# Another order for the steps of the attention in a one-core decoder kernel

## The chip, the cores and the metric

The kernel runs on one core of a Trainium2 chip, in one launch. The metric is the device time of the program in microseconds (us). The five instruction streams that matter are TensorE (PE, matmuls; PEld is its weight load), VectorE (DVE), ScalarE (ACT), GpSimd (POOL) and SyncE (SP, which only issues transfers). Each takes its instructions in the order in which they stand in its queue, and an instruction whose input or buffer isn't ready holds up all that stand behind it.

## The reference, cut to what matters

A decoder trunk of two layers over 256 tokens of width 1024, in float32. Each layer has a feed-forward network (FFN) before and after a mixer, each followed by a LayerNorm. The mixer of the first layer is a gated recurrence, that of the second an attention in which 16 heads of width 64 look back in three dilated windows (groups). All three groups share one key and one value; each has its own query. The change touches only this attention:

```
q = (x @ w_q).reshape(bsz, s, N_GROUPS, N_HEADS, HEAD_DIM)
for g, (window, dilation) in enumerate(DILATION_PAIRS):
    o, l = dilated_group(q[:, :, g], k, v, slopes, window, dilation)   # softmax over the window's keys
    outs.append(o); lses.append(l)
wts = softmax(stack(lses, axis=0), axis=0)
out = sum(wts[..., None] * stack(outs, axis=0), axis=0)
return out.reshape(bsz, s, N_HEADS * HEAD_DIM) @ w_o
```

The weighted sum over the three groups is the same as one softmax over the keys of all three, and so the kernel computes it: exps of three groups, one sum, one division.

## The kernel before

All weights come from memory in pieces of 128x1024 float32 (512 KB). A piece is loaded into a tile `raw`, and is then split into a rounded part `w_hi` (line 127, a cast on ScalarE) and the remainder `w_lo` (line 128, on VectorE); each product is made of three matmuls, hi x hi, hi x lo, lo x hi (line 90). There are 4 buffers for `raw` and 10 for the split pieces. `pump` (line 139) loads and splits the next piece, `take` (line 145) hands out the oldest split one.

The attention runs over 8 pairs of heads. It is written as steps, and the text `ATTENTION` (line 620) names them in order; a step is a letter and a number. Inside the attention ScalarE, VectorE and GpSimd keep this order (`pinned`, line 152), and so do all matmuls (line 88): the text alone says in which order each engine meets its work.

| step | what it does | engine, line |
|---|---|---|
| `pv` | next weight piece: transfer, cast, remainder (`pV`: the cast on VectorE too) | SP 126, ACT 127, DVE 128 |
| `r` | transposes the first queries, which were projected for two pairs at once | PE 98, ACT 665 |
| `U` n | query projection of pair n/3, group n mod 3: 24 matmuls, 128x256 | PE 88 |
| `Q` n | scales it and keeps it (frees U's bank) | ACT 665 |
| `F` p, `S` p | scores of pair p for the first and the second 128 tokens: 6 matmuls each | PE 88 |
| `M` h | adds the distances to the scores of head h and finds the extremum (frees the banks of F and S) | DVE 717 |
| `E` h | exp, with its sum | ACT 726 |
| `N` h | reciprocal of the sum; adds the three groups | DVE 733 to 735 |
| `L` h | scales by the reciprocal (`sg`, `hh`) | ACT 743 |
| `P` h, `C` h | three transposes; keeps their result (frees P's bank) | PE 98, DVE 754 |
| `O` p, `D` p | value sums of pair p, 4 matmuls; splits them in `o_hi` and `o_lo` (frees O's bank) | PE 88, ACT 104, DVE 105 |
| `J` n | a quarter of the output projection for one piece of `w_o`: 6 matmuls | PE 88 |

A head goes through F, S, M, E, N, L, P, C, and a pair then through O and D. Between them TensorE makes the query projections of later pairs, and behind the last of those the parts J. The results of U, F, P, O (and half of the last S) take a bank each of the four named `mm`; the two double banks `yy` hold S, and from J0 on the output projection.

`T` at the end of the text gives the numbers of pieces that are issued in `finish` (line 279), which computes the rest of the projection with the LayerNorm: the first ahead of it, the second behind the first add of the LayerNorm (line 237), the third behind its scaling (lines 249 and 250). Then the LayerNorm's rows are transposed (line 254), split into `xT` (lines 104, 105), and the last FFN begins.

Of the kernel before, what the change touches and what calls it, by code (L numbers as in the profile page):

```python
# [46 lines left out]
def trunk_kernel(  # L47
# [397 lines left out]
    def natural_pair(turn_x, then):  # L445


        later = []
        for t, ps in enumerate(natural_both(turn_x)):
            tmp = act.tile([P, 512], F32, name="nat", tag="o_hi", bufs=4)  # L450
            nc.scalar.copy(tmp, ps)

            def rest(t=t, tmp=tmp):
                pt = bank()
                for m in range(4):
                    turn(pt[:, m * P:(m + 1) * P], tmp[:, m * P:(m + 1) * P])
                then(t, pt.rearrange("p (m s) -> p m s", m=4))
            later.append(rest)
        return later
# [157 lines left out]
    def kv_duo():  # L617
        return [act.tile([P, 2, SEQ], F32R, name="kv", bufs=KVBUFS) for _ in range(2)]

    ATTENTION = """pv pV U2 Q2 pv r0 pv r1 U5 Q5 F0 S0 U6 M0 pv pv E0 N0 M1 U7 L0 P0 E1 Q7 pv U8 N1 C0 Q6 F1 S1 U9 L1 M2  # L620
        pv E2 P1 U10 C1 Q8 M3 O0 N2 E3 N3 L2 Q10 U11 P2 pv D0 C2 pv F2 S2 L3 M4 Q11 E4 Q9 N4 U12 L4 P3 C3 U13
        O1 U14 Q12 M5 E5 pv pv pv N5 P4 L5 F3 S3 C4 Q13 D1 M6 U15 pv E6 P5 Q14 C5 U16 M7 O2 Q15 pv E7 N6 L6
        U17 P6 N7 L7 D2 pv Q17 F4 S4 C6 M8 pv P7 Q16 E8 C7 U18 N8 L8 M9 Q18 pv O3 E9 U19 D3 pv F5 S5 P8 N9 C8
        L9 Q19 U20 M10 P9 Q20 E10 C9 N10 M11 U21 pv L10 U22 Q21 pv P10 E11 Q22 N11 C10 U23 O4 pv F6 S6 pv pv
        D4 M12 Q23 pv E12 N12 L11 L12 P11 C11 M13 J0 O5 pv P12 J4 E13 N13 C12 D5 L13 F7 S7 P13 J3 M14 E14 J7
        N14 L14 C13 O6 J11 M15 E15 P14 C14 N15 J8 pv J2 D6 L15 P15 J1 C15 O7 J6 pv J5 D7 T20100""".split()
    ATTENTION_TAIL = ((3, 0), (2, 1), (3, 1)), ((3, 1), (2, 0), (3, 0))

    def keys_values(turn_x):
# [23 lines left out]
    def attention(kv, ln_i, turn_x):  # L653
# [134 lines left out]
        rest = natural_pair(turn_x, first)  # L788
        for s in ATTENTION:
            if s[0] == "p":  # L790
# [115 lines left out]
```

## Time and profile before

| | us |
|---|---|
| three runs | 1064.87, 1065.18, 1067.47 (median 1065.18) |
| profiled execution | 1063.59 |
| its span, first to last instruction | 1061.5 |
| TensorE busy | 1033.7 (97%) |
| VectorE busy | 649.8 (61%) |
| ScalarE busy | 525.5 (50%) |
| GpSimd busy | 11.9 (1%) |

The profile is of one execution; 2.1 us of it lie around the span. Matmuls overlap, so a busy TensorE isn't TensorE at its peak. The attention (from U2 to the transposes of its LayerNorm) lies at 737 to 864 us of the span. In a timeline a row gives the start, the time that the instructions took, the engine, the line, the operation with output and inputs, and in brackets how long the engine sat idle before it and which instruction ended that. In the chain of waits, which is followed back from the last instruction, a row is a start, a length and what the program's end hung on.

### The profile page before, as it was taken

What the parts mean: (1) busy time and instruction counts of PE and PEld (TensorE: products, weight loads), DVE (VectorE), ACT (ScalarE), POOL (GpSimd) and SP (SyncE); (2) the same over time, 40 slices, a digit from 0 to 9 for tenths busy, and PEclk for the clock granted to TensorE, in tenths of its full rate; (3) what the DMA queues carried; (4) which work ended last, traced back from release to release, by engine and by line L of the source; (5) the groups of instructions that cost most, each with busy time, mean ns of one, the idle gap of its engine ahead of it and who ended that gap; (6) DMA issues with size and microseconds to landing.
All of it is one profiled execution on the core that took longest, in us unless ns stands there. A gap on an engine that the chain in (4) does not pass through costs nothing.

```text
span 1061.5 us, 13737 instructions
## 1 busy us (share of the span) xinstructions
PE 1033.7 (97%) x5305; PEld 869.0 (82%) x5305; DVE 649.8 (61%) x847; ACT 525.5 (50%) x730; POOL 11.9 (1%) x18
## 2 busy tenths in 40 slices
PE   9999999999899999999999999999998889999997
PEld 7888888899778888887988888888888778888885
DVE  5765555685886455557645545557776887554544
ACT  6664443369745444343534444433765745443430
POOL 0000000000000000000000000000000000000000
PEclk9999999999999999999999999999999999999999
DMA  8885555185358565652856555461432547555521
GB/s 295 279 290 184 198 176 182 65 281 183 113 197 274 177 198 172 205 176 90 295 183 216 182 189 197 160 199 54 146 121 99 179 139 266 203 178 206 179 99 40
DMA packets 55648, 192.69 MB, mean 182 GB/s; under 512 B 6432, under 2 KB 6688, under 8 KB 55584
## 3 DMA queue, kind: packets, MB, share of 16 engines
q1 hardware_dynamic: 55584, 191.83, 53.4%
q8 instruction: 41, 0.67, 0.3%
q14 instruction: 23, 0.19, 0.1%
HBM read 190.75 MB, written 1.05 MB: 181 GB/s over the span
## 4 chain that ended last, share of the span: by engine, by line
PE 85%; ACT 6%; DVE 6%; issue 1%; DMA 1%; POOL 0%; SPq 0%; DVEq 0%; ACTq 0%; POOLq 0%
PE mm L88 54%; PE yy L88 28%; PE mm L98 3%; DVE w_lo L128 2%; ACT w_hi L127 2%; ACT sc L726 1%; ACT th L101 1%; ACT L101 1%; DMA raw<-in_q_w_dram 0%; DVE sc L717 0%; DMA raw<-in_w_in_dram 0%; DVE sc L735 0%; DVE xn L237 0%; ACT aa L101 0%; DVE st L238 0%
## 5 line engine op out<-in xcount | busy, mean ns | idle before, releaser
L128 DVE TENSOR_TENSOR w_lo<-raw,w_hi 128x1024 fp32r<-128x1024 f32 (+1 forms) x343 | 413.5, 1220 | 222.1 <-ACT w_hi L127 212.1
L88 PE MATMUL mm<-w_hi,xT 128*128 128x512 f32 x1536 | 494.2, 394 | 1.8 <-DVE xT L105 1.8
L127 ACT CAST w_hi<-raw 128x1024 fp32r<-128x1024 f32 (+1 forms) x342 | 354.2, 1049 | 238.5 <-PE yy L88 112.1
L88 PEld LDWEIGHTS mm<-w_hi,xT 128*128 128x128 f32 x1536 | 288.5, 188 | 63.6 <-DVE xT L105 3.8
L88 PE MATMUL mm<-w_lo,xT 128*128 128x512 f32 x768 | 299.8, 390 | 1.0 <-DVE w_lo L128 1.0
L88 PEld LDWEIGHTS mm<-w_lo,xT 128*128 128x128 f32 x768 | 144.5, 188 | 30.8 <-DVE w_lo L128 2.1
L88 PE MATMUL yy<-w_hi,h_hi 128*128 128x512 f32 x352 | 138.3, 393 | 0.0
L88 PE MATMUL yy<-w_hi,h_lo 128*128 128x512 f32 x352 | 137.2, 390 | 0.0
L88 PE MATMUL yy<-w_lo,h_hi 128*128 128x512 f32 x352 | 137.0, 389 | 0.0
L347 ACT ACTIVATE sg<-mm 128x256 f32<-128x256 f32 x88 | 33.7, 383 | 153.7 <-PE mm L88 153.3
L350 DVE SCALAR_TENSOR_TENSOR gated<-mm,sg 128x256 f32<-128x256 f32 x88 | 36.8, 420 | 106.6 <-ACT sg L347 106.6
L88 PE MATMUL mm<-xT,w_hi 128*128 128x256 f32 x480 | 89.9, 289 | 2.8 <-ACT q L665 2.6
L88 PEld LDWEIGHTS mm<-xT,w_hi 128*128 128x128 f32 x480 | 75.7, 194 | 5.3 <-ACT q L665 2.8
L88 PEld LDWEIGHTS yy<-w_hi,h_lo 128*128 128x128 f32 x352 | 66.1, 188 | 13.9
L88 PEld LDWEIGHTS yy<-w_lo,h_hi 128*128 128x128 f32 x352 | 66.2, 188 | 13.3
L88 PEld LDWEIGHTS yy<-w_hi,h_hi 128*128 128x128 f32 x352 | 66.1, 188 | 13.3
L88 PE MATMUL mm<-xT,w_lo 128*128 128x256 f32 x240 | 68.5, 285 | 0.0
L88 PEld LDWEIGHTS mm<-xT,w_lo 128*128 128x128 f32 x240 | 46.5, 194 | 0.0
L104 ACT CAST xT<-mm 128x512 fp32r<-128x512 f32 x20 | 11.7, 586 | 60.4 <-PE mm L98 60.3
L88 PE MATMUL yy<-xT,w_hi 128*128 128x256 f32 x224 | 41.2, 286 | 0.0
L105 DVE TENSOR_TENSOR h_lo<-mm,h_hi 128x512 fp32r<-128x512 f32 x44 | 30.3, 689 | 13.0 <-ACT h_hi L104 13.0
L88 PEld LDWEIGHTS yy<-xT,w_hi 128*128 128x128 f32 x224 | 35.1, 192 | 0.2
(109 smaller groups left out, 709.8 us busy)
## 6 DMA issues: line engine op xcount, KB each, us to landing
raw<-in_w_in_dram SPq DMA_DIRECT2D x175, 512.0 KB, 4.5
raw<-in_w_out_dram SPq DMA_DIRECT2D x88, 512.0 KB, 5.0
raw<-in_q_w_dram SPq DMA_DIRECT2D x20, 512.0 KB, 4.0
raw<-in_rg_in_dram SPq DMA_DIRECT2D x16, 512.0 KB, 4.9
gb<-in_ln_dram SPq DMA_DIRECT2D x24, 256.0 KB, 5.9
raw<-in_rg_out_dram SPq DMA_DIRECT2D x10, 512.0 KB, 4.0
raw<-in_v_w_dram SPq DMA_DIRECT2D x8, 512.0 KB, 4.8
raw<-in_k_w_dram SPq DMA_DIRECT2D x8, 512.0 KB, 5.3
```

The source lines that it names most:

```text
L88: tc.keep_in_program_order(nc.tensor.matmul(ps, lhsT=lhsT, rhs=rhs, start=start, stop=stop))
L98: tc.keep_in_program_order(nc.tensor.transpose(ps, src, ident))
L101: tc.keep_in_program_order(nc.scalar.activation(dst_, src, f, **kw))
L104: nc.scalar.copy(hi, src)
L105: nc.vector.tensor_tensor(lo, src, f32(hi), ALU.subtract)
L127: (nc.scalar.copy if high is nc.scalar else high.tensor_copy)(w[0][:, c], raw[:, c])
L128: i = low.tensor_tensor(out=w[1][:, c], in0=raw[:, c], in1=f32(w[0][:, c]), op=ALU.subtract)
L347: nc.scalar.activation(sg, ps[:, :256], AF.Silu)
L350: nc.vector.scalar_tensor_tensor(gated[j][:, t, :], ps[:, 256:], 0.5, sg, ALU.mult, ALU.mult)
L726: nc.scalar.activation(scs[h][:, :, c], scs[h][:, :, c], AF.Exp, bias=mns[h][:, t, 1:2], scale=-1.0, accum_out=den[:, t:t + 1])
```

## The change

Only the text of steps and the three numbers behind `T` change. The text has 209 steps before and after, among them the same 27 `pv` and one `pV`. No function changes.

```
-    ATTENTION = """pv pV U2 Q2 pv r0 pv r1 U5 Q5 F0 S0 U6 M0 pv pv E0 N0 M1 U7 L0 P0 E1 Q7 pv U8 N1 C0 Q6 F1 S1 U9 L1 M2
...
-        N14 L14 C13 O6 J11 M15 E15 P14 C14 N15 J8 pv J2 D6 L15 P15 J1 C15 O7 J6 pv J5 D7 T20100""".split()
+    ATTENTION = """pv pV U2 pv r0 r1 U5 Q2 F0 S0 U6 M0 pv pv E0 N0 U7 M1 Q5 pv pv L0 E1 P0 N1 C0 Q7 U8 F1 S1 Q6 U9 L1 M2
...
+        P13 J7 N14 C13 L14 J11 O6 P14 J8 C14 J2 D6 E15 N15 pv J1 L15 P15 C15 J5 pv O7 J6 D7 T12000""".split()
```

At `T` the pieces are 2, 0 and 1 before, and 1, 2 and 0 now. On TensorE few steps move: P3 stands ahead of U12, U20 ahead of P8, F6 ahead of U23, with S6 still behind O4, and at the end J4, J7, J11, J1 and J5 a place or two from where they were. SyncE and GpSimd keep their order. Most of what moves stands on ScalarE and VectorE. Three places:

ScalarE around L9, the scaling of head 9 (its exps are `sc_6876` before and `sc_6866` now; `q_6895` before and `q_6891` now are U19's query). Before:

```order
L726 ACTIVATE sc_6876,den_6892<-sc_6876,mn_6877 128x3x256
L104 CAST o_hi_6793<-mm_6887 128x256
L127 CAST w_hi_6924<-raw_6923 128x1024
L743 ACTIVATE sg_6955<-sc_6876,rd_6949 128x128
L743 ACTIVATE hh_6956<-sc_6876,rd_6949 128x256
L665 ACTIVATE q_6895<-mm_6896,qsc_104 128x256
L665 ACTIVATE q_6960<-mm_6961,qsc_104 128x256
L726 ACTIVATE sc_6986,den_6995<-sc_6986,mn_6987 128x3x128
L726 ACTIVATE sc_6986,den_6995<-sc_6986,mn_6987 128x3x256
```

And now:

```order
L726 ACTIVATE sc_6866,den_6888<-sc_6866,mn_6867 128x3x256
L104 CAST o_hi_6795<-mm_6877 128x256
L127 CAST w_hi_6966<-raw_6965 128x1024
L743 ACTIVATE sg_6971<-sc_6819,rd_6862 128x128
L743 ACTIVATE hh_6972<-sc_6819,rd_6862 128x256
L743 ACTIVATE sg_6983<-sc_6866,rd_6961 128x128
L743 ACTIVATE hh_6984<-sc_6866,rd_6961 128x256
L665 ACTIVATE q_6933<-mm_6934,qsc_104 128x256
L726 ACTIVATE sc_6979,den_6994<-sc_6979,mn_6980 128x3x128
L726 ACTIVATE sc_6979,den_6994<-sc_6979,mn_6980 128x3x256
L665 ACTIVATE q_6891<-mm_6892,qsc_104 128x256
```

L8 moved down to L9, Q20 ahead of E10, and Q19 behind E10.

ScalarE around E11 and E12, the exps of heads 11 and 12 (`sc_7004` and `sc_7160` before, `sc_7060` and `sc_7160` now). Before:

```order
L726 ACTIVATE sc_7004,den_7081<-sc_7004,mn_7005 128x3x256
L665 ACTIVATE q_7044<-mm_7045,qsc_104 128x256
L127 CAST w_hi_7123<-raw_7122 128x1024
L127 CAST w_hi_7145<-raw_7144 128x1024
L127 CAST w_hi_7151<-raw_7150 128x1024
L104 CAST o_hi_7156<-mm_7117 128x256
L665 ACTIVATE q_7091<-mm_7092,qsc_104 128x256
L127 CAST w_hi_7166<-raw_7165 128x1024
L726 ACTIVATE sc_7160,den_7171<-sc_7160,mn_7161 128x3x128
L726 ACTIVATE sc_7160,den_7171<-sc_7160,mn_7161 128x3x256
L743 ACTIVATE sg_7178<-sc_7004,rd_7085 128x128
L743 ACTIVATE hh_7179<-sc_7004,rd_7085 128x256
```

And now:

```order
L726 ACTIVATE sc_7060,den_7080<-sc_7060,mn_7061 128x3x256
L665 ACTIVATE q_7034<-mm_7035,qsc_104 128x256
L665 ACTIVATE q_6997<-mm_6998,qsc_104 128x256
L127 CAST w_hi_7100<-raw_7099 128x1024
L127 CAST w_hi_7132<-raw_7131 128x1024
L743 ACTIVATE sg_7137<-sc_7060,rd_7083 128x128
L743 ACTIVATE hh_7138<-sc_7060,rd_7083 128x256
L127 CAST w_hi_7155<-raw_7154 128x1024
L665 ACTIVATE q_7105<-mm_7106,qsc_104 128x256
L127 CAST w_hi_7166<-raw_7165 128x1024
L127 CAST w_hi_7172<-raw_7171 128x1024
L726 ACTIVATE sc_7160,den_7177<-sc_7160,mn_7161 128x3x128
```

L11 (`sg` and `hh` from E11's exps) moved from behind E12 to ahead of it; two casts now stand directly ahead of E12, and D4 has gone from there.

VectorE at the same place, from the second half of M12 on (`p_7190` before and `p_7196` now are C11's result). Before:

```order
L717 ISA sc_7160,mn_7161<-yy_7136,dst_103 128x3x256
L717 ISA mn_7161 128x1
L128 TENSOR_TENSOR w_lo_7167<-raw_7165,w_hi_7166 128x1024
L733 RECIPROCAL rd_7174<-den_7171 128x2
L734 TENSOR_TENSOR sc_7160<-sc_7160 128x384
L735 TENSOR_TENSOR sc_7160<-sc_7160 128x384
L754 COPY p_7190<-mm_7186 128x384
L717 ISA sc_7192,mn_7193<-mm_7129,dst_103 128x3x128
L717 ISA mn_7193 128x1
L717 ISA sc_7192,mn_7193<-yy_7137,dst_103 128x3x256
```

And now:

```order
L717 ISA sc_7160,mn_7161<-yy_7146,dst_103 128x3x256
L717 ISA mn_7161 128x1
L128 TENSOR_TENSOR w_lo_7167<-raw_7165,w_hi_7166 128x1024
L128 TENSOR_TENSOR w_lo_7173<-raw_7171,w_hi_7172 128x1024
L733 RECIPROCAL rd_7180<-den_7177 128x2
L734 TENSOR_TENSOR sc_7160<-sc_7160 128x384
L735 TENSOR_TENSOR sc_7160<-sc_7160 128x384
L717 ISA sc_7184,mn_7185<-mm_7089,dst_103 128x3x128
L717 ISA mn_7185 128x1
L717 ISA sc_7184,mn_7185<-yy_7147,dst_103 128x3x256
L717 ISA mn_7185 128x1
L754 COPY p_7196<-mm_7192 128x384
```

A second remainder stands ahead of N12, and C11 moved behind M13.

## Rows read from the trace of the kernel before

**Rows 1.** The page's part 1: busy us (share of the span), instructions.

```profile
PE 1033.7 (97%) x5305; PEld 869.0 (82%) x5305; DVE 649.8 (61%) x847; ACT 525.5 (50%) x730; POOL 11.9 (1%) x18
```

**Rows 2.** Timeline of TensorE, 745 to 850 us, rows with idle time.

```profile
753.17 0.33 PE L98 MATMUL mm<-ident,sg 128*128 128x128 f32 x1 [0.68 <-ACT sg L743]
...
785.21 0.48 PE L88 MATMUL mm<-k,q 64*128 64x128 f32 x2 [2.06 <-DVE p L754]
...
799.52 0.71 PE L88 MATMUL mm<-k,q 64*128 64x128 f32 x8 [0.38 <-ACT q L665]
...
814.17 0.51 PE L88 MATMUL mm<-xT,w_hi 128*128 128x256 f32 x2 [2.57 <-ACT q L665]
...
833.75 0.33 PE L98 MATMUL mm<-ident,sg 128*128 128x128 f32 x1 [2.67 <-ACT sg L743]
```

**Rows 3.** Chain of waits, 740 to 862 us: start, us, what.

```profile
742.48 4.82 DMA raw<-in_q_w_dram
...
753.51 1.52 ACT sc L726 x4
...
786.02 0.82 PE mm L88 x9
786.84 1.41 PE yy L88 x10
788.25 3.08 PE mm L88 x24
...
814.17 4.39 PE mm L88 x24
...
852.86 7.05 PE yy L88 x30
```

**Rows 4.** One window: engines' busy us (instructions), then the granted clock, DMA share, GB/s.

```profile
816.00:817.00 1.00, 1.00 (x6) 1.00 (x6) 0.00 (x0) 0.00 (x0) 0.00 (x0) 0.50 0.00 0
```

**Rows 5.** Timeline around the attention's LayerNorm, 859 to 869 us.

```profile
863.78 0.63 PE L98 MATMUL mm<-ident,xn 128*128 128x128 f32 x4 [1.16 <-DVE xn L250]
...
865.00 1.22 DVE L128 TENSOR_TENSOR w_lo<-raw,w_hi 128x1024 fp32r<-128x1024 f32 x1
...
868.18 0.73 PE L88 MATMUL mm<-w_hi,xT 128*128 128x512 f32 x2 [1.49 <-DVE xT L105]
```

**Rows 6.** Timeline ahead of F3, 778 to 786 us.

```profile
779.00 2.94 ACT L127 CAST w_hi<-raw 128x1024 fp32r<-128x1024 f32 x3
780.07 3.50 DVE L128 TENSOR_TENSOR w_lo<-raw,w_hi 128x1024 fp32r<-128x1024 f32 x3 [2.03 <-ACT w_hi L127]
783.48 0.16 DVE L733 RECIPROCAL rd<-den 128x2 f32<-128x2 f32 x1
...
784.61 0.55 DVE L754 COPY p<-mm 128x384 f32<-128x384 f32 x1
```

**Rows 7.** Timeline ahead of U20, 811 to 815 us.

```profile
812.96 0.40 ACT L743 ACTIVATE sg<-sc,rd 128x128 f32<-128x128 f32 x1 [2.48 <-DVE sc L735]
...
813.25 0.55 DVE L717 CUSTOM_DVE_ANT_1 sc<-mm,dst 128x384 f32<-128x384 f32 x1
...
813.67 0.45 ACT L665 ACTIVATE q<-mm,qsc 128x256 f32<-128x256 f32 x1
...
814.60 0.08 DVE L717 DVE_READ_ACCUMULATOR2_ANT mn<- 128x1 f32 x1
```

**Rows 8.** Timeline around E0, 745 to 755 us.

```profile
747.45 0.08 DVE L717 DVE_READ_ACCUMULATOR2_ANT mn<- 128x1 f32 x1
...
748.44 1.28 ACT L726 ACT_TABLE_LOAD   x1
749.74 0.62 ACT L726 ACTIVATE sc<-sc,mn 128x384 f32<-128x384 f32 x1
```

**Rows 9.** Timeline ahead of P11, 825 to 835 us: N11's second add, and L11.

```profile
826.24 0.56 DVE L735 TENSOR_TENSOR sc<-sc 128x384 f32<-128x384 f32 x1
...
833.31 0.39 ACT L743 ACTIVATE sg<-sc,rd 128x128 f32<-128x128 f32 x1
```

More of the change, by code (lines that the diff above doesn't have):

```diff
@@ L618, in kv_duo @@
         return [act.tile([P, 2, SEQ], F32R, name="kv", bufs=KVBUFS) for _ in range(2)]
-    ATTENTION = """pv pV U2 Q2 pv r0 pv r1 U5 Q5 F0 S0 U6 M0 pv pv E0 N0 M1 U7 L0 P0 E1 Q7 pv U8 N1 C0 Q6 F1 S1 U9 L1 M2
[L621 to L625, printed above, removed]
-        N14 L14 C13 O6 J11 M15 E15 P14 C14 N15 J8 pv J2 D6 L15 P15 J1 C15 O7 J6 pv J5 D7 T20100""".split()
+    ATTENTION = """pv pV U2 pv r0 r1 U5 Q2 F0 S0 U6 M0 pv pv E0 N0 U7 M1 Q5 pv pv L0 E1 P0 N1 C0 Q7 U8 F1 S1 Q6 U9 L1 M2
+        pv P1 E2 U10 Q8 M3 C1 O0 Q9 E3 U11 N2 N3 pv L2 Q10 P2 D0 pv C2 F2 S2 L3 P3 M4 E4 N4 Q11 M5 U12 C3 U13
+        pv L4 O1 U14 E5 P4 pv Q13 pv F3 N5 D1 S3 Q12 C4 M6 pv L5 U15 P5 U16 E6 M7 pv E7 C5 O2 N6 U17 Q15 N7
+        L6 P6 pv Q14 D2 L7 F4 S4 M8 P7 Q16 Q17 C6 E8 C7 U18 N8 M9 pv Q18 O3 pv E9 U19 F5 S5 U20 D3 N9 pv L8
+        P8 M10 L9 Q20 C8 P9 E10 U21 C9 Q19 N10 L10 U22 M11 pv pv P10 E11 N11 Q22 F6 C10 Q21 pv U23 pv L11 O4
+        S6 pv M12 Q23 pv pv E12 N12 M13 L12 P11 C11 D4 J0 J4 P12 O5 C12 E13 F7 S7 N13 D5 L13 J3 M14 M15 E14
+        P13 J7 N14 C13 L14 J11 O6 P14 J8 C14 J2 D6 E15 N15 pv J1 L15 P15 C15 J5 pv O7 J6 D7 T12000""".split()
     ATTENTION_TAIL = ((3, 0), (2, 1), (3, 1)), ((3, 1), (2, 0), (3, 0))
```

## The prediction

> **What bounds the kernel now.** I read the page's busy shares first: TensorE is busy 97% of the span [rows 1], so over the whole program little can be won. The change touches one stage, the attention, at 737 to 863 us. Second, therefore, the timeline of TensorE alone in that stage: every row with an idle time names what ended it. Between U2 and the last O there are nine such rows, 0.68, 0.20, 0.24, 2.06, 0.32, 0.38, 2.57, 2.67 and 0.19 us, in all 9.3 us; the ones that matter most stand in [rows 2]. Each costs some 0.25 us more than its idle time, since the array has to fill again (in the chain of waits step follows step without that loss [rows 3]): 9 x 0.25 = 2.3. [...] So the stage loses 9.3 + 2.3 + 1.3 = 12.9 us to its order. That is all that another order can win there; at its end 1.16 and 1.49 us more are lost around the LayerNorm [rows 5].
>
> **Durations for the sum**, start to start. TensorE: F 0.8, S 1.4, U 3.0 [rows 3], P 0.3; J is 6 of 30 matmuls in 7.05 us [rows 3], 1.4 to 1.5 with its start; O 0.8, as F. ScalarE: cast 0.98 (three in 2.94) [rows 6], E 1.52 [rows 3], L 0.71 (812.96 to 813.67) and Q 0.45 [rows 7]. VectorE: remainder 1.16 (three in 3.50), N 1.13 (783.48 to 784.61), C 0.5 [rows 6], M 1.43 (813.25 to 814.68) [rows 7]; D I take at 0.4, less than C, whose tile is larger. A weight piece lands 4.8 us after its raw buffer is free [rows 3].
>
> **The change part by part.** It adds and removes no instruction: casts, exps, matmuls and transfers are the same in number, and SP and POOL keep their rows. Only places move, so each term is a wait that goes or comes.
>
> Start (P0). Before, the sixth cast stood ahead of E0 and waited for its transfer until 747.3 [rows 3]; the table load and E0 came behind it [rows 8], and P0 waited 0.68 us. Now E0 stands ahead of that cast and starts when M0 ends (747.53 [rows 8]) and the table is there, about 747.7, two us earlier; two casts that go between E0 and L0 take the time back only partly (L0 at 751.5, not 752.7). P0 follows U7 at 752.3 without a wait: -1.2 with the second half of the transposes, which was late too. As E0, M1 and C0 come earlier, the small waits of U9 (0.20) and F2 (0.24) go as well: -0.7.
> The trace shows 1.28 us of table load and E0 0.02 us behind it [rows 8]. [...]
>
> F3 (2.06 and 0.32, in all 3.1 with filling). Before, it waited for a bank that C4 gave back: C4 stood behind three remainders and N5. Now D1 is put ahead of C4, and D1 gives the second bank. Counted from the end of M5: C3 0.5 and the first remainder to 1.7; the second follows a cast behind E5 (0.1 + 1.52 + 0.98 = 2.6) and ends at 3.8, the third at 4.95, N5 at 6.1, D1 at 6.45. TensorE has U13's rest 1.15, O1 0.8, U14 3.0, P4 0.3 = 5.25. So 1.2 us of waiting stay: -1.9. F4 (0.38): Q14 now stands ahead of D2, -0.6.
>
> U20 (2.57, filling and clock: 4.1 in all). It waited for the bank of Q19, which stood behind L9, and L9 waited for N9 [rows 7]. Now U20 stands ahead of P8 and takes the bank of O3, which D3 gives back some 1.5 us before: -4.1. Q19 moves behind E10, so the next banks are late: P9 waits for Q20 (0.35) and U21 for C8 (0.2): +0.55.
>
> P11 (2.67, with filling 3.1). N11's second add ended at 826.80, but L11 started only at 833.31 [rows 9]: it stood behind Q22, four casts, D4, Q23 and E12. Now L11 stands behind two casts only and ahead of E12; it ends 3 us before P11 wants it: -3.1. F6 is drawn ahead of U23, and its second bank comes from Q22, behind E11: +0.65.
>
> The last pairs, new waits. From the end of S6 (time 0): M12's second half ends at 0.95 and gives J0 its banks, TensorE is done with P11 at 0.3: +0.7. J0 and J4 end at 3.8. E12 now stands behind two casts, the second of which has its transfer at about 1.3 (its raw buffer is freed by a remainder 3.5 us before S6's end, and 4.8 us pass): cast to 2.3, E12 to 3.8, N12 to 5.0, L12's parts to 5.4 and 5.8. P12: +1.7. M13 stands ahead of C11: 5.0 + 1.43 + 0.47 = 6.9, TensorE waits with O5 from 6.05: +0.85. Behind P12 and O5 on TensorE stand F7 and S7, and M14 to C15 wait for those, so these waits reach the end in full. From F7 on VectorE and ScalarE keep ahead (O6 wants C13 at 14.7 and has it at 14.5, so its 0.19 goes, -0.4, by a margin of 0.2).
>
> The other moves I cost at nothing: P3 ahead of U12 and J1, J5 and J6 change places with steps whose inputs are over 1 us old, and a weight piece is still split five U steps (15 us) ahead of the U that takes it; if that cover were gone, a piece would cost its lateness at its U.
>
> Tail. One weight piece is issued ahead of the last projection and two behind its first quarter, where it was two and one. Two remainders (2.3) now lie between the two adds of the first LayerNorm, where VectorE had 1.3 free: the transposes wait 1.0 longer (+1.0 on the 1.16). In return the remainder at 865.00, which held back the xT that TensorE waited 1.49 for [rows 5], is gone from there: -1.1. Together 0.
>
> **Sum.** Waits that go: 1.2 + 0.7 + 3.1 + 0.6 + 4.1 + 3.1 + 0.4 = 13.2 (12.9 by the rows, the difference is rounding). Waits that come or stay: 1.2 + 0.55 + 0.65 + 0.7 + 1.7 + 0.85 = 5.65. Net 12.9 - 5.65 = 7.2, say -7 us. The profiled execution took 1063.6; it would take 1056.6. The median of the runs is 1.6 above it, so I predict 1065.2 - 7 = 1058.2. Bounds: no new wait at all gives -13 (1052); if each of the eleven places where a margin is under 0.5 us fails by 0.5, -7 + 5.5 = -1.5 (1063.7).
>
> **Rivals.**
> A. The gaps only move. Five of the nine waits are for a PSUM bank, there are still four, and the order of TensorE hardly changes. For it: F3, F6, P9 and U21 still wait in my own count. The price: if every bank wait returns in its old size, only P0, L11's and the clock's terms stay, 1.2 + 3.1 + 1.3 = 5.6, less the new chain waits 0.7 + 1.7 + 0.85 = 3.25: -2.4, 1062.8, which measures as no change (this kernel can tell 0.3%, 3.2 us). Against it: at U20 the bank was held by a place in a queue [rows 7], not by a lack of time. [...]
> B. Better: the chain at P12 and O5 is shorter than counted because the second transfer is in time (-1.0 at P12, and with it O5) and F3's cast is not late (-1.2): -9.5 to -10, 1055.5. Against: the cast at P0 waited for exactly such a transfer [rows 3].
> C. Slower: casts that wait for their transfers hold up the exps. The new order puts two casts ahead of each of E11, L11 and E12, and one ahead of the second xT cast in the tail. Four places; if a transfer takes x us instead of 4.8, each loses x - 4.8. It eats the gain of 7 at x = 6.6 and costs 3.2 us more than before from x = 7.4 on; at 7.6 the time is 1069.4. For it: transfers queue where four are freed at once. Against: 4.8 us was seen with the queue in use [rows 3].
> D. A new stop brings the clock down as after U20: +1.3 each. P12 and the LayerNorm's transposes now stop 1.7 and 2.2 us; stops of 2.06 and 2.67 us [rows 2] did not bring it down, so I count none; one would make 1059.5, within my own case.
>
> **How the numbers follow.** My forecast (1055.5 to 1061): 0.58. A (1061 to 1065): 0.20. B (under 1055.5): 0.12. C and whatever else ends above 1065: 0.10. Faster by over 0.3% (below 1062): all of mine and B, and a little under half of A: 0.58 + 0.12 + 0.08 = 0.78. Same: the rest of A and a part of C, 0.15. Slower 0.07. For 8 in 10 I leave out the slower cases and the best end: 1053.5 to 1064.
>
> **What would show it.** In the timeline of the changed kernel: P0, U20 and P11 without an idle time over 0.3 us; no stretch at 0.50 in the attention; F3 still waiting 1 to 1.5 us for VectorE's o_lo; P12 about 1.7 us for ScalarE; the wait ahead of the LayerNorm's transposes near 2.2 us, and the one behind them near 0.4. Wrong would be: casts waiting for a transfer over 1 us ahead of E11 or E12 (C), or TensorE's idle time in the stage still over 8 us (A).

## The result and the profile after

The changed kernel took 1055.45 us (median of 4 runs, 1054.36 to 1057.09), the kernel before on the same chip 1066.33 (4 runs, 1064.87 to 1067.88): ratio 0.990, 95% interval 0.988 to 0.992, or 10.9 us less. The prediction said 1058.2 (8 in 10: 1053.5 to 1064.0), faster. The profiled execution took 1054.88 us, its span is 1052.8: 8.7 us under that of before.

Part 1 of the page shows the same work in a shorter span [rows 1]:

```profile
PE 1033.1 (98%) x5305; PEld 867.1 (82%) x5305; DVE 650.5 (62%) x847; ACT 524.9 (50%) x730; POOL 11.9 (1%) x18
```

Timeline of TensorE, 738 to 860 us: all rows with an idle time (in brackets, with what ended it).

```profile
809.68 0.33 PE L98 MATMUL mm<-ident,sg 128*128 128x128 f32 x1 [0.24 <-ACT q L665]
...
817.14 0.93 PE L88 MATMUL mm<-k,q 64*128 64x128 f32 x10 [0.28 <-ACT q L665]
...
824.48 0.50 PE L88 MATMUL yy<-w_hi,o_hi 128*128 128x512 f32 x1 [0.57 <-DVE mn L717]
...
828.75 0.33 PE L98 MATMUL mm<-ident,sg 128*128 128x128 f32 x1 [1.25 <-ACT sg L743]
...
853.12 0.50 PE L88 MATMUL yy<-w_hi,o_hi 128*128 128x512 f32 x1 [0.29 <-DVE xn L237]
...
856.23 0.63 PE L98 MATMUL mm<-ident,xn 128*128 128x128 f32 x4 [1.45 <-DVE xn L250]
...
859.50 0.73 PE L88 MATMUL mm<-w_hi,xT 128*128 128x512 f32 x2 [0.35 <-DVE xT L105]
```

The first four are P9, F6, J0 and P12, the last three lie in the tail. Up to the last O the stops add up to 2.34 us where nine came to 9.3 [rows 2]; P0, U9, F2 to F4, U20 and P11 have no such row, and no window of 1 us from 736 to 870 has a granted clock under 0.99 (before: 0.50 behind U20's stop [rows 4]). From U2's start to the first FFN matmul that waited (859.50; before 868.18 [rows 5]) the traces give 121.34 us against 130.58: 9.24 less. U2 itself started 0.56 us later.

Chain of waits, 781 to 853 us: start, us, what.

```profile
781.47 1.17 PE mm L88 x11
782.63 1.41 PE yy L88 x10
...
819.67 4.68 DMA raw<-in_o_w_dram
824.37 1.05 ACT w_hi L127
825.42 1.54 ACT sc L726 x4
...
850.13 2.34 DVE w_lo L128 x2
```

The first two rows are F3 and S3, 2.58 us together; before F3 took 0.82 behind its stops and S3 1.41 [rows 3]. The next three are what P12 waits for: transfer, second cast, E12. The last is the pair of remainders between the adds of the first LayerNorm.

Timeline of ScalarE at E0 and L0, then of VectorE ahead of F3's second bank:

```profile
746.10 1.28 ACT L726 ACT_TABLE_LOAD   x1
747.39 0.62 ACT L726 ACTIVATE sc<-sc,mn 128x384 f32<-128x384 f32 x1
...
751.59 0.40 ACT L743 ACTIVATE sg<-sc,rd 128x128 f32<-128x128 f32 x1 [0.17 <-DVE sc L735]
```

```profile
775.62 0.08 DVE L717 DVE_READ_ACCUMULATOR2_ANT mn<- 128x1 f32 x1
...
777.76 2.54 DVE L128 TENSOR_TENSOR w_lo<-raw,w_hi 128x1024 fp32r<-128x1024 f32 x2 [0.45 <-ACT w_hi L127]
...
781.34 0.42 DVE L105 TENSOR_TENSOR o_lo<-mm,o_hi 128x256 fp32r<-128x256 f32 x1
```

E0 starts 0.01 us behind the end of the table load, before 0.02 [rows 8]. D1's remainder ends at 781.76, 6.06 us behind M5's end (775.70); TensorE came for the bank at 781.4.

### The profile page after: what moved, and what is told of

The parts are those of the page before. It is cut to its first block, busy times and chain, and to the rows that moved or that the text cites. A ratio compares the mean times of both kernels' runs of the same rounds, so it can differ in the third digit from the quotient of the medians.

```text
span 1052.8 us, 13746 instructions
## 1 busy us (share of the span) xinstructions
PE 1033.1 (98%) x5305; PEld 867.1 (82%) x5305; DVE 650.5 (62%) x847; ACT 524.9 (50%) x730; POOL 11.9 (1%) x18
## 3 DMA queue, kind: packets, MB, share of 16 engines
HBM read 190.75 MB, written 1.05 MB: 182 GB/s over the span
## 4 chain that ended last, share of the span: by engine, by line
PE 89%; ACT 4%; DVE 4%; DMA 1%; issue 1%; POOL 0%; SPq 0%; DVEq 0%; ACTq 0%; POOLq 0%
PE mm L88 57%; PE yy L88 29%; PE mm L98 3%; DVE w_lo L128 1%; ACT w_hi L127 1%; ACT th L101 1%; ACT L101 1%; DVE xn L237 0%; DMA raw<-in_w_in_dram 0%; DMA raw<-in_o_w_dram 0%; ACT sc L726 0%; DVE xn L250 0%; ACT aa L101 0%; DVE st L238 0%; DVE xT L105 0%
## 5 line engine op out<-in xcount | busy, mean ns | idle before, releaser
L350 DVE SCALAR_TENSOR_TENSOR gated<-mm,sg 128x256 f32<-128x256 f32 x88 | 36.9, 420 | 105.7 <-ACT sg L347 105.5
```

The costliest lines, as they stand in the source:

```text
L350: nc.vector.scalar_tensor_tensor(gated[j][:, t, :], ps[:, 256:], 0.5, sg, ALU.mult, ALU.mult)
```

## Experiments

Numbers of steps are places in the `ATTENTION` text; after steps 42, 103, 143 and 208 both texts have issued the same steps, so that a stretch can be exchanged. "Dip" is a stretch in which the windows show a granted clock down to 0.50.

### Stretch by stretch

Start alone:

```
-old[1..42]  old[43..208] T20100
+new[1..42]  old[43..208] T20100
```

> The old order with only its start exchanged (the first 42 steps, U2 to O0, as in the changed kernel; the rest as before). My count: P0 waits no longer (-1.2), nor does U9 (-0.25 or so); nothing later depends on it. From U2's start to O0's start 26.4 us instead of 27.9, whole time -1.5 us. Rival (gaps only move): the 1.5 us come back as a longer wait at F2 or F3 (before 0.24 and 2.06 us), whole time unchanged.

Measured: 1064.42 us, ratio 0.997 (0.996 to 0.998), -3.2 us. In its trace U2 to O0 takes 26.46 us, as counted (before 27.94), and F2 with S2 2.47 us instead of 2.88; F3's 2.06 us stayed as they were. So nothing is handed on to F2 or F3 as the rival had it; a small part is handed on further back, where P11's stop is 3.08 us instead of 2.67. The median fell by more than the count; the dips, below, are the place to look, but which of them this order avoids I have not separated.

F2 to F4 alone:

```
-old[1..42] old[43..103] old[104..208] T20100
+old[1..42] new[43..103] old[104..208] T20100
```

> The old order with only steps 43 to 103 exchanged (E3 to Q15's neighbourhood: F2, F3, F4). My count: F2 -0.45, F3 -1.9, F4 -0.6, together -3.0 us; by the changed kernel's trace, where F3 does not stop, -4.2 us from O0 to P7. Rival (four PSUM banks set the pace, gaps only move): F3 and F4 stop in the sum about as long as before (2.76 us idle) or the stop at U20 grows beyond its 2.57 us by what is won here, whole time within 1 us of before.

Measured: 1062.61 us, ratio 0.995 (0.994 to 0.996), -5.5 us. O0 to P7 takes 32.28 us instead of 36.14, none of F2, F3 and F4 stops, and U20's stop is 2.29 us, not longer. The four PSUM banks do not set the pace here.

U20's stretch alone:

```
-old[1..103] old[104..143] old[144..208] T20100
+old[1..103] new[104..143] old[144..208] T20100
```

> The old order with only steps 104 to 143 exchanged (U20 ahead of P8, Q19 behind E10). My count: -4.1 at U20, of it 1.3 us the clock, which has no stop of over 0.5 us to fall behind; +0.55 at P9 and U21: -3.6 us, U20 in 3.1 us at a granted clock of 1.00. Rival (gaps only move): only the clock's 1.3 us are won, idle time of TensorE from P7 to U22 stays over 2 us.

Measured: 1063.92 us, ratio 0.997 (0.995 to 0.998), -3.7 us. P7 to U22 takes 16.46 us instead of 20.20, with one stop left (P9, 0.24). But this execution shows a dip that the one of before did not have. Windows of 1 us of it, TensorE alone (length, TensorE's busy us and instructions, then the granted clock, DMA share, GB/s):

```profile
788.00:789.00 1.00, 1.00 (x10) 0.56 0.89 274
789.00:790.00 1.00, 1.00 (x9) 0.50 0.67 274
```

It lies behind F3's stop, which is untouched (2.06 and 0.32 us), and F3's remaining matmuls with S3 took 3.90 us instead of 2.23: 1.67 us more.

The last pairs alone:

```
-old[1..143] old[144..208] T20100
+old[1..143] new[144..208] T20100
```

> The old order with only steps 144 to 208 exchanged (the last two pairs), tail as before. My count: -3.1 at P11, -0.4 at O6, +0.65 at F6, +0.7 at J0, +1.7 at P12, +0.85 at O5: +0.4 us, that is no change, because the wait at P11 only turns into the waits at J0 and P12. Rival (the L11 step was the whole price and the new waits are hidden in the old context): -2 to -3 us.

Measured: 1066.54 us, ratio 0.999 (0.998 to 1.001): no change, as counted. P11's stop is gone, and these came (timeline of TensorE, rows with idle time at J0 and P12):

```profile
835.69 0.50 PE L88 MATMUL yy<-w_hi,o_hi 128*128 128x512 f32 x1 [0.57 <-DVE mn L717]
...
840.44 0.33 PE L98 MATMUL mm<-ident,sg 128*128 128x128 f32 x1 [1.69 <-ACT sg L743]
```

Behind P12's 1.69 us the clock fell here:

```profile
842.00:843.00 1.00, 1.00 (x7) 0.50 1.01 406
```

F3's stretch put back into the changed kernel:

```
-new[1..42] new[43..103] new[104..208] T12000
+new[1..42] old[43..103] new[104..208] T12000
```

> The changed kernel with steps 43 to 103 in the old order: only F2's, F3's and F4's stops come back. By the traces' difference from O0 to P7 +4.2 us; by my count of the prediction +3.0. With the clock theory a dip behind F3 in most executions makes it +5.5 to +6, as the splice the other way (-5.2 by medians) had it. Rival (parts are not additive, the rest of the new order absorbs the stop): under +2.5 us.

Measured: 1062.28 us, ratio 0.995 (0.994 to 0.997), against 0.990 for the changed kernel: 5 to 7 us lost by this one stretch. The stop has its old size, and a dip behind it (timeline, then a window):

```profile
784.42 0.49 PE L88 MATMUL mm<-k,q 64*128 64x128 f32 x2 [2.06 <-DVE p L754]
```

```profile
787.00:788.00 1.00, 1.00 (x8) 0.50 0.23 94
```

Its runs spread from 1060.19 us at a mean clock of 0.995 to 1063.71 at 0.992. Parts add up from this side too. The four stretches alone, -3.2, -5.5, -3.7 and nothing that can be measured, make some -12.4 us where all together give -10.9; each has an interval of over 1 us to either side, so the sum is as good as that.

The tail put back:

```
-... O7 J6 D7 T12000
+... O7 J6 D7 T20100
```

> The changed kernel with the old tail (two weight pieces ahead of the last projection, one behind the first quarter's scale). The prediction counted the tail's move at 0: +1.0 at the transposes, -1.1 at the second xT. By the traces the two waits of before are 1.16 + 1.49 = 2.65, after 0.29 + 1.45 + 0.35 = 2.09: so here +0.3 to +0.6 us, within what can be measured. Rival (the old tail is better behind the new order, since its remainder between the adds is gone): -0.5 us or less.

Measured: 1056.43 us (1055.65 to 1058.96), ratio 0.990 (0.989 to 0.992): no difference that can be measured. The timeline has 1.16, 0.18 and 1.05 us of stops, 2.39 in all against 2.09:

```profile
857.22 0.63 PE L98 MATMUL mm<-ident,xn 128*128 128x128 f32 x4 [1.16 <-DVE xn L250]
...
859.85 0.50 PE L88 MATMUL mm<-w_hi,xT 128*128 128x512 f32 x1 [0.18 <-ACT xT L104]
...
861.63 0.73 PE L88 MATMUL mm<-w_hi,xT 128*128 128x512 f32 x2 [1.05 <-DVE xT L105]
```

### One step at a time

Q19 ahead of L9:

```
-... C8 L9 Q19 U20 ...
+... C8 Q19 L9 U20 ...
```

> The old order with one swap: Q19 ahead of L9 instead of behind it. My count: Q19 need not wait for N9 and L9, its bank comes about 1.8 us earlier, U20's stop falls from 2.57 to about 0.8 us and the 1.3 us of clock behind it go: -3.3 us, nearly all that the change won at this place. Rival (the bank is late for another reason, TensorE's own order): U20's stop stays over 2 us and nothing is won.

Measured: 1065.37 us (12 runs, 1064.59 to 1066.25), ratio 0.998 (0.997 to 0.999), -2.2 us. U20's stop is gone altogether, not down to 0.8, and P7 to U22 takes 15.83 us: one word in the text does at this place as much as the forty exchanged steps (16.46). By the runs it won less than they did, and less than the 3.3 expected: its mean clock is 0.989 to 0.992, theirs 0.993 to 0.995. Stops at F3 (2.06) and P11 (2.96) stayed, and both have a dip behind them in this execution.

L11 ahead of the casts:

```
-... U23 O4 pv F6 S6 pv pv D4 M12 Q23 pv E12 N12 L11 L12 P11 ...
+... U23 L11 O4 pv F6 S6 pv pv D4 M12 Q23 pv E12 N12 L12 P11 ...
```

> The old order with one step moved: L11 up from behind E12 and N12 to behind U23, ahead of the four casts. Count: P11's stop of 2.67 us goes with its filling (-3.1), and P12, which waited for nothing, may now be late, as E12 and N12 stand where they stood and TensorE arrives 3 us earlier: +1 to +2. Net -1 to -2 us, and by the clock theory the dip behind P11 goes, or comes behind P12 instead, which leaves the clock of the runs at 0.992 to 0.993. Rival (the whole stop is won, 3.1 and the clock's 1.5): -4.5 us.

Measured: 1067.98 us, ratio 1.001 (1.000 to 1.002): nothing won. Both expectations fell; P12 was not the next to be late, J0 was. Timelines of TensorE (P11, J0) and of VectorE ahead of it:

```profile
833.80 0.33 PE L98 MATMUL mm<-ident,sg 128*128 128x128 f32 x1 [0.42 <-ACT q L665]
...
836.48 0.50 PE L88 MATMUL yy<-w_hi,o_hi 128*128 128x512 f32 x1 [2.13 <-DVE mn L717]
```

```profile
831.25 3.50 DVE L128 TENSOR_TENSOR w_lo<-raw,w_hi 128x1024 fp32r<-128x1024 f32 x3 [1.40 <-ACT w_hi L127]
834.66 0.42 DVE L105 TENSOR_TENSOR o_lo<-mm,o_hi 128x256 fp32r<-128x256 f32 x1
...
835.47 0.95 DVE L717 CUSTOM_DVE_ANT_0 sc<-yy,dst 128x768 f32<-128x768 f32 x1
```

J0 needs the double bank `yy` that M12 (835.47) gives back, and M12 stands behind three remainders and D4. F6's start to J0's start is 5.33 us, with P11's stop it was 5.50. Two queues held the same place, ScalarE's L11 and VectorE's M12; the changed text moves both, M12 ahead of two of the casts and ahead of D4.

E12 ahead of the cast:

```
-... Q23 pv pv E12 N12 ...
+... Q23 pv E12 pv N12 ...
```

> The changed kernel with one swap: E12 ahead of the second of the two casts that stood before it. The cast waited for its transfer until 824.37; without it E12 starts when M12 ends (824.4 for its second half, 823.5 for its first), about 1 us earlier, and P12's stop of 1.25 us falls to 0.3: -1.0 us, with its filling and O5 -1.5. Rival (the chain M12, E12, N12, L12 is what is late, not the cast): P12 stops 1 us or more, no change.

Measured: 1058.15 us, ratio 0.991 (0.989 to 0.994): no gain, and P12 stops longer. One timeline, of three engines: ScalarE's second cast behind E12, VectorE's remainder and N12, TensorE's P12:

```profile
827.38 1.03 ACT L127 CAST w_hi<-raw 128x1024 fp32r<-128x1024 f32 x1
...
828.45 1.23 DVE L128 TENSOR_TENSOR w_lo<-raw,w_hi 128x1024 fp32r<-128x1024 f32 x1 [0.90 <-ACT w_hi L127]
...
829.59 0.16 DVE L733 RECIPROCAL rd<-den 128x2 f32<-128x2 f32 x1
...
831.35 0.33 PE L98 MATMUL mm<-ident,sg 128*128 128x128 f32 x1 [1.87 <-ACT sg L743]
```

E12 did end 1.5 us earlier (2.0 us behind S6's end instead of 3.5). But `pv` is a cast and a remainder, and the remainder still stood ahead of N12 on VectorE, now waiting for a later cast. I had moved an instruction on one engine and not looked at its twin.

### The stops and the clock

The same order as with Q19 moved, with matmuls into the stops; `fill` multiplies parts of xT into a bank that is written over afterwards:

```
+ if p == 3:                       # in first_scores: S3's bank, taken early
+     early.append(two_banks()); fill(early[0], 16)
+ if h == 11:                      # in turn_p: P11's own bank
+     fill(pt, 20)
```

> As the run with Q19 ahead of L9, and TensorE is given work that changes no result while it waits: 16 matmuls of 256 columns ahead of F3 and 20 ahead of P11, some 2.0 and 2.4 us by U's 0.122 us each. They are written over afterwards. Theory (a stop of over 2 us also lowers the granted clock behind it in most executions, 1.4 to 1.7 us each, seen behind F3's, U20's and P11's stops in single runs): clock stays 1.00 through the attention, mean clock of the runs 0.995 to 0.996, median 1.5 to 3 us below the run without the fill. Rival (the clock falls for another reason, the stops cost their idle time alone): same time as without the fill, or up to 0.5 us longer, dips of the clock as often as there.

Measured: 1061.91 us (7 runs, 1061.15 to 1062.48), ratio 0.995 (0.993 to 0.997). Without the fill it was 1064.59 to 1066.25: 36 matmuls more, and 3.5 us less. The mean clock of the runs is 0.994 to 0.995, where it was 0.989 to 0.992; 0.995 to 0.996 was expected. Timeline of TensorE with the fill, at F3 and P11:

```profile
785.38 2.15 PE L88 MATMUL yy<-xT 128*128 128x256 f32 x16
787.69 0.48 PE L88 MATMUL mm<-k,q 64*128 64x128 f32 x2 [0.15 <-DVE p L765]
...
829.12 2.65 PE L88 MATMUL mm<-xT 128*128 128x256 f32 x20
832.15 0.33 PE L98 MATMUL mm<-ident,sg 128*128 128x128 f32 x1 [0.38 <-ACT sg L752]
```

The waits kept their length: P4's start to F3's is 2.55 us in both, F6's start to P11's 5.19 without and 5.20 with the fill. The difference is in the windows behind them (no window from 730 to 875 us is under 1.00 with the fill), first without it, then with it:

```profile
789.00:790.00 1.00, 1.00 (x7) 0.50 0.54 221
...
835.00:836.00 1.00, 1.00 (x4) 0.50 0.94 379
```

```profile
789.00:790.00 1.00, 1.00 (x15) 1.00 0.77 270
...
835.00:836.00 1.00, 1.00 (x10) 1.00 1.04 340
```

So the stop costs its idle time and, in many executions, a dip. Over all profiled executions here F3's unfilled stop of 2.06 and some 0.3 us has a dip behind it in 5 of 7, U20's (2.29 to 2.58) in 3 of 5, P11's (2.67 to 3.08) in 3 of 5; P12's at 1.69 and 1.87 in both, at 1.25 to 1.33 in none of 3; J0's 2.13 in its one. Why one and the same stop has a dip in one execution and not in another is open.

The kernel before is longer at the lower clock in most executions than in the profiled one. Of its 54 executions in the three comparisons 8 have a mean clock of 0.995 and took 1063.8 to 1064.5 us; 46 have 0.989 to 0.993 and took 1066.2 to 1071.2. The profiled one (1063.59, 0.995) is of the rarer kind, with one dip in the attention. A dip like F3's (3.4 us at half, by the windows) is 0.0016 of the mean clock, so the usual execution, 3.4 us longer and 0.003 lower, has about two such lengths more; that is worked out, since none of these was profiled, and a mean clock does not say where they lie. They need not both lie in the attention. Two dips outside it, near 274 us and at the program's end, are in every trace, and the one near 274 us is 3.4 us long in five of the fourteen (before, changed, and three others) and 6.8 in nine. One window of it, in the kernel before and in the run with Q19 moved:

```profile
277.00:278.00 1.00, 1.00 (x6) 1.00 0.00 0
```

```profile
277.00:278.00 1.00, 1.00 (x3) 0.50 0.00 0
```

In the five U2 starts at 738.6 us on average, in the nine at 739.9. So one of the two lengths can be there. The two runs with and without the fill both have the long one, so it does not disturb that comparison of traces.

### A better order of the last pairs

```
-... L11 O4 S6 pv M12 Q23 pv pv E12 N12 M13 L12 P11 C11 D4 J0 ...
+... L11 S6 O4 pv M12 Q23 pv E12 P11 N12 M13 C11 pv L12 D4 J0 ...
```

> The changed kernel with another order of the last pairs: O4 behind S6, E12 ahead of the second of its two casts, and that cast with its remainder behind N12, M13 and C11 on VectorE. Count: J0 finds M12 done, 0.57 goes; E12 ends 2.0 us behind S6, N12 3.3, L12 4.2, TensorE reaches P12 at 4.1: its 1.25 go; O5 needs C11 at 5.1 and TensorE comes at 4.7: 0.4 of 0.55 stay. With filling -2.3 us. Rival (what the swap of E12 alone showed: another instruction queued on VectorE takes the cast's place): P12 stops 1 us or more, no change.

Measured: 1054.70 us (1053.86 to 1055.40), ratio 0.988 (0.987 to 0.990). J0 and P12 no longer stop; one stop is left from J0 to the last O, because D4's remainder now stands behind the moved one:

```profile
831.07 0.82 PE L88 MATMUL mm<-k,q 64*128 64x128 f32 x9 [0.19 <-DVE o_lo L105]
```

U23's start to the LayerNorm's transposes takes 36.9 us instead of 38.2, so 1.3 of the 2.3 counted came: O5 still runs 1.42 us instead of 0.87, since C11 ends at 829.55 and O5 starts at 829.05.

With the tail in a third way as well:

```
-... O7 J6 D7 T12000
+... O7 J6 D7 T21000
```

> As the run before, and the tail in a third way: two weight pieces ahead of the last projection, one between the two adds of the first LayerNorm. Only one remainder lies between the adds then: the second add starts 0.85 us earlier, the stop of 0.29 goes and 0.3 to 0.6 of the 1.45. Against the run before -0.6 us, against the changed kernel -2.9 us. Rival (the first add is pushed back by the second remainder ahead of it): against the run before 0 to +0.5.

Measured: 1054.52 us (1053.75 to 1054.64), ratio 0.988 (0.987 to 0.990): against the run before no difference that can be measured. By the traces 0.4 of the 0.6 counted came: the stop of 0.29 us is gone, the other two are as they were:

```profile
855.96 0.63 PE L98 MATMUL mm<-ident,xn 128*128 128x128 f32 x4 [1.44 <-DVE xn L250]
...
859.24 0.73 PE L88 MATMUL mm<-w_hi,xT 128*128 128x512 f32 x2 [0.36 <-DVE xT L105]
```

This is the lowest median here. On the same chip the changed kernel with the old tail took 1056.43; the interval of the ratio overlaps that of the changed kernel (0.988 to 0.992), so what the new order wins over that one (1.7 us by the traces, U23's start to the FFN) is not shown by the runs.

## Why the prediction was right, and where it was off

Its frame held: the gain lies in the attention alone, it is waits of TensorE that go, and parts add up (rival A fell in both exchanges of F3's stretch; six, not five, of the nine rows were waits for a bank, as F3 has two, and with four banks as before none of the six is left). The size was low: 7 us counted, 10.9 measured, so that the time lies inside the wide range but just below the forecast's own part (1055.5 to 1061). By place, counted and measured between the two traces, in us:

| place | counted | measured |
|---|---|---|
| P0, U9 | -1.45 | -1.48 |
| F2, F3, F4 | -2.95 | -4.16 |
| U20 with the clock, P9, U21 | -3.55 | -3.72 |
| F6, P11, J0, P12, O5, O6 | +0.4 | +0.39 |
| tail | 0 | -0.24 |
| sum | -7.5, called -7 | -9.2 |

- **F3 was mis-sized.** "1.2 us of waiting stay": 0.41 stayed (F3 and S3 2.58 us instead of 2.17). I started the chain at M5's end, but E5's first half starts on M5's first half, so the cast, the remainders and N5 came 0.4 to 0.6 us earlier, and P4 ended at 5.7 instead of 5.25. The 0.25 us of filling that I added at F2 and F4 is what the starts ahead of F3 show in the trace before: 2.44 us from the transposes of `hh` (782.77) to F3 (785.21), where 0.13 lie behind the same transposes at 775.71 that nothing stops, so 2.31 lost for 2.06 idle; a stop inside F, with two matmuls ahead of it, cost 0.47 beyond its idle time (F2 and S2 2.88 instead of 2.17 us with 0.24 idle).
- **The last pairs came out term by term**: J0 +0.8 (0.7 counted), P12 +1.7 (1.7), O5 +0.55 (0.85), F6 +0.85 (0.65). The transfer of E12's second cast was late as counted: ScalarE waited 1.79 us for it. The prediction had named a cast that waits over 1 us there as a sign of rival C, and its own sum held that wait; the sign was badly chosen. The transfer took 4.68 us, not more than the 4.8 counted, and that is why C fell. Pieces issued close together did take longer in the trace before: three, issued at 781.32, 782.46 and 783.59, landed after 3.7, 5.4 and 5.6 us. That it was late at all is against the first of rival B's reasons; the second, that F3's cast is not late, held for 0.8 of its 1.2 us. That B's 1055.5 us is the time that came is luck in part: F2, F4 and the clock, none of them in B, made up for what B had wrong.
- **The tail's 0** was -0.24 by the traces, and nothing in the runs. Ahead of the transposes stand 1.45 us and 0.29 earlier, not the 2.2 that the prediction named; behind them 0.35 (0.4 named).
- **The clock is the term that failed.** Its 1.3 us at U20 came with the trace before: 4.39 us where a U takes 3.08 [rows 3], at a granted clock of 0.50 [rows 4]. "Stops of 2.06 and 2.67 us did not bring it down, so I count none": true of the one execution that was profiled. In others the same stops have a dip behind them, which cost 1.40 us behind P11 with the start alone and 1.67 behind F3 with U20's stretch alone, and the fill shows that the stop is the cause; the trace of the changed kernel has none in the attention. The usual execution of the kernel before has, by its mean clock, about two lengths of dip more than the profiled one, of which one can lie near 274 us. The prediction carried the 1.6 us between profiled execution and median over to the changed kernel; the runs have 2.7 before and 0.6 after. So they gave 10.9 us where the traces gave 8.7 and the sum 7. That dips behind these stops are what went is shown for the runs with and without the fill; for the 2.2 us between runs and traces it is the likely cause, not shown. Rival D looked for new dips after the change; they were in the kernel before.

## What to carry to other kernels

Price a stop of the bounding engine by its idle time and by what the clock loses behind it (1.40 and 1.67 us in the two dips above), and compare the mean clock of several runs with that of the profiled one before taking its dips as all there are; it tells how much is lost, not where. Before a step is moved up, list everything that its place is waiting for: where two queues hold it, moving one wins nothing, and a step that issues on two engines has to be followed on both. Order is cheap to try one word at a time: in the traces one swap won all that the change won at U20.

## What the runs showed of the hardware

Work that nobody needs can make a kernel faster: 36 matmuls put into two stops took 3.5 us off, since the granted clock stayed at 1.00 instead of falling to 0.50, in the profiled execution for 3.4 us behind the one and 6.8 behind the other. The traces show a dip behind waits for ScalarE (U20's 2.29 to 2.58 us, P11's 2.96 to 3.08) and for VectorE (F3's 2.06, J0's 2.13), down to a stop of 1.69 us (0.50 behind it), and not always (F3's stop in 5 of 7).
